# Row sums on one core: the first 2048 rows as two contiguous blocks, each with its own load and store

## The chip, the cores and the metric

One core of a Trainium2 chip. The metric is device time of one execution in microseconds (us). An execution counts as slow when it is over 1.5% above the fastest of its kernel, and else as fast. A profile's span is some 1.8 us shorter than the time, because the time also counts what lies around the program.

A load or a store is cut into packets, pieces that one of 16 DMA engines moves one after another. An instruction of SyncE or ScalarE issues it, and semaphores report its end.

## The reference

```python
batch, seq, dim = 32, 512, 1024
x = np.random.randn(batch, seq, dim).astype(np.float32)      # 67.1 MB
def reference(x):
    return np.sum(x, axis=-1).astype(np.float32)             # 16384 sums, 64 KB
```

There are 16384 rows of 4 KB. Each is read once, so the kernel is a stream of loads with a short head and a short tail.

## The kernel before

Rows are taken in groups of 2048: partition p of group g holds 16 neighbouring rows, one 64 KB run. VectorE sums most of them; near the end ScalarE takes some, and the last row comes in two pieces. The parts that matter here:

```python
BIG = 16
x_g = x.flatten_outer_dims().rearrange("(g p j) d -> g p j d", p=P, j=BIG)
out_v = out.rearrange("b s -> (b s)").rearrange("(g p j) -> p g j", p=P, j=BIG)
def rows_from(j, n):
    return x_g[j // BIG, :, j % BIG : j % BIG + n, :]
# ... (cut)
last = J // BIG - 1
FIRST = 4
# ... (cut)
        for g in range(last):
            t = inpool.tile([P, BIG * dim + 4], fp32)
            if g == 0:
                rows(t, 0, FIRST, 0, 0)                       # first load: 4 rows per partition
                first = sums_of[-1]
                rows(t, FIRST, BIG - FIRST, FIRST, 0)         # second load: the other 12
                continue
# ... (cut: the last group in pieces; `two` is the load of two rows per partition)
        hold(store(nc.scalar, 0, last), two, "its packets come behind those of the loads")
        halves(whole[:, :1], part)
        halves(sums[:, j : j + 1], whole)
        store(nc.sync, last, last + 1)
```

The first two loads together fill group 0, so each reads 128 runs (16 KB, then 48 KB) that start 64 KB apart; I call that distance the pitch. One store from ScalarE's queue writes the sums of the first seven groups, one from SyncE's queue those of the last. At the close SyncE waits for the ScalarE store, all engines meet at a barrier, and GpSimd, which also waits for the last store, clears the semaphores.

## Time and profile before

| | |
|---|---|
| time, median of 3 runs | 162.1 us (161.92 to 162.17) |
| span of the profiled execution | 159.6 us (its time was 161.4) |
| loads' queue, share of 16 DMA engines | 97.8% |
| first load landed | 7.14 us |
| last load landed, then end of span | 157.43 us, 2.2 us later |

### The profile page before, as it was taken

How to read it: one execution, taken by the hardware profiler on the slowest of the kernel's cores; microseconds unless marked ns; L12 is line 12 of the kernel's file. 1: busy time of each engine (PE TensorE's matmuls, PEld its weight loads, DVE VectorE, ACT ScalarE, POOL GpSimd, SP SyncE). 2: the span in 40 equal slices, each digit the busy share in tenths (PEclk: the TensorE clock that was granted, in tenths of full speed). 3: DMA queues.
4: the chain of work that ended last, by engine and by line, in shares of the span. 5: the costliest groups of instructions: out<-in, count | busy, mean ns of one | idle time of the engine just before them, and what ended most of it. 6: DMA issues, size and time to landing. Idle time of an engine off the chain costs nothing.

```text
span 159.6 us, 125 instructions
## 1 busy us (share of the span) xinstructions
DVE 120.1 (75%) x22; ACT 17.3 (11%) x31; POOL 0.2 (0%) x4
## 2 busy tenths in 40 slices
DVE  0290059960799958999499994999949999497953
ACT  3000000000000000000000000000000000496953
POOL 0000000000000000000000000000000000000000
DMA  7999996996996989979969969969969969798984
GB/s 263 460 406 579 394 526 263 526 526 263 526 526 263 526 378 411 526 312 476 526 279 509 526 263 526 526 263 526 526 263 526 509 279 526 337 452 371 467 365 128
DMA packets 2928, 67.18 MB, mean 421 GB/s; under 512 B 1264, under 2 KB 1392, under 8 KB 1520
## 3 DMA queue, kind: packets, MB, share of 16 engines
q1 hardware_dynamic: 2016, 67.12, 97.8%
q10 hardware_dynamic: 912, 0.06, 0.4%
HBM read 67.11 MB, written 0.07 MB: 421 GB/s over the span
## 4 chain that ended last, share of the span: by engine, by line
DMA 73%; DVE 25%; SPq 1%; issue 0%; DVEq 0%
DMA t<-in_x_dram 73%; DVE sums L141 24%; SPq L180 1%; SPq L221 0%; DVE t L155 0%; DVEq L252 0%
## 5 line engine op out<-in xcount | busy, mean ns | idle before, releaser
L141 DVE TENSOR_REDUCE sums<-t 128x16 f32<-128x16384 f32 (+3 forms) x9 | 116.6, 12954 | 35.3 <-DMA t<-in_x_dram 35.3
L168 ACT ACTIVATE unread<-t 128x1024 f32<-128x1024 f32 x15 | 15.2, 1012 | 139.2 <-DMA t<-in_x_dram 139.2
L155 DVE CUSTOM_DVE_ANT_0 t<-t 128x512 f32<-128x512 f32 (+2 forms) x6 | 3.5, 602 | 2.4 <-DMA t<-in_x_dram 2.4
L168 ACT ACTIVATION_READ_ACCUMULATOR unread<-t 128x1 f32 x15 | 2.8, 187 | 0.0
L168 ACT ACT_TABLE_LOAD x1 | 1.3, 1283 | 0.8 <-PEq L241 0.8
L155 DVE DVE_READ_ACCUMULATOR2_ANT sums<- 128x1 f32 x5 | 0.4, 83 | 0.0
L241 POOL MEMSET const-uint8-127<- 128x1 uint8 x1 | 0.1, 102 | 0.0
L241 POOL MEMSET const-bfloat16-1.0<- 128x1 bf16 x1 | 0.1, 101 | 0.0
L241 POOL MEMSET const-float32-0.0<- 128x1 f32 x1 | 0.1, 98 | 0.2 <-issue 0.2
L241 POOL MEMSET const-float32-1.0<- 128x1 f32 x1 | 0.1, 98 | 0.0
L155 DVE DVE_READ_ACCUMULATOR2_ANT t<- 128x1 f32 x1 | 0.1, 81 | 0.0
L219 DVE MEMSET t<- 128x1 f32 x1 | 0.1, 59 | 0.0
## 6 DMA issues: line engine op xcount, KB each, us to landing
t<-in_x_dram SPq DMA_DIRECT2D x1, 6144.0 KB, 20.9
t<-in_x_dram SPq DMA_DIRECT2D x1, 4096.0 KB, 31.1
t<-in_x_dram SPq DMA_DIRECT2D x1, 2560.0 KB, 36.9
t<-in_x_dram SPq DMA_DIRECT2D x1, 2048.0 KB, 7.1
t<-in_x_dram SPq DMA_DIRECT2D x1, 1024.0 KB, 38.9
t<-in_x_dram SPq DMA_DIRECT2D x1, 280.0 KB, 39.1
t<-in_x_dram SPq DMA_DIRECT2D x1, 232.0 KB, 39.2
t<-in_x_dram SPq DMA_DIRECT2D x6, 40.8
```

Source lines behind the costliest of these rows:

```text
L141: return nc.vector.tensor_reduce(out=dst, in_=src, axis=mybir.AxisListType.X, op=mybir.AluOpType.add)
L155: return nc.vector.tensor_tensor_reduce(out=src[:, :n], in0=src[:, :n], in1=src[:, n:], scale=1.0, scalar=0.0, op0=mybir.AluOpType.add, op ...
L168: nc.scalar.activation(out=unread[:, :n], in_=src, func=mybir.ActivationFunctionType.Copy, accum_out=dst,)
L180: load = nc.sync.dma_start(out=block, in_=rows_from(j, n))
L219: nc.vector.memset(whole[:, width + 1 :], 0.0)
L241: nc = _bacc.Bacc("TRN2", target_bir_lowering=False, num_devices=1)
```

## The change

The intent is that the first two loads read memory in one piece each: 4 neighbouring rows per partition in the first 512 rows, then 12 per partition in the next 1536. Their sums then belong to other places of the output, so the ScalarE store must be split in three. (`FIRST = 4` only moved up; `x_g` and `out_v` are the lines of before, written with `x_r` and `out_r`. The lines they replace are cut.)

```diff
+    FIRST = 4
+    x_r = x.flatten_outer_dims()
+    out_r = out.rearrange("b s -> (b s)")
+    x_g = x_r.rearrange("(g p j) d -> g p j d", p=P, j=BIG)
+    out_v = out_r.rearrange("(g p j) -> p g j", p=P, j=BIG)
+    blocks = ((0, FIRST), (FIRST, BIG - FIRST))
+    x_0 = [x_r[a * P : (a + n) * P].rearrange("(p j) d -> p j d", j=n) for a, n in blocks]
+    out_0 = [out_r[a * P : (a + n) * P].rearrange("(p j) -> p j", j=n) for a, n in blocks]
 
     def rows_from(j, n):
+        if j < BIG:
+            return x_0[blocks.index((j, n))]
         return x_g[j // BIG, :, j % BIG : j % BIG + n, :]
...
-        hold(store(nc.scalar, 0, last), two, "its packets come behind those of the loads")
+        behind = "its packets come behind those of the loads"
+        for (r, n), dst in zip(blocks, out_0):
+            hold(nc.scalar.dma_start(out=dst, in_=sums[:, r : r + n]), two, behind)
+        hold(store(nc.scalar, 1, last), two, behind)
```

More of the change, by code (lines that the diff above doesn't have):

```diff
@@ L117 @@
     BIG = 16
-    x_g = x.flatten_outer_dims().rearrange("(g p j) d -> g p j d", p=P, j=BIG)
-    out_v = out.rearrange("b s -> (b s)").rearrange("(g p j) -> p g j", p=P, j=BIG)
+    FIRST = 4
[6 more added lines that the diff above has]
+    out_0 = [out_r[a * P : (a + n) * P].rearrange("(p j) -> p j", j=n) for a, n in blocks]
     def rows_from(j, n):
+        if j < BIG:
+            return x_0[blocks.index((j, n))]
         return x_g[j // BIG, :, j % BIG : j % BIG + n, :]
     last = J // BIG - 1
-    FIRST = 4
     pieces = (560, 464)
```

## The prediction

> **What bounds the kernel now.** I read the page first (busy shares, the 40 slices, the DMA queues), then the chain of waits in order of time, then the waits, then groups by form, then the timeline of the last five microseconds, and at last the trace's single records of packets and of semaphore increments, because the change touches only the first and the last few microseconds.
>
> The page, parts 1 to 4: VectorE is busy 75% of the span, ScalarE 11%, while the loads' queue takes 97.8% of what 16 DMA engines have in the span. The chain that ends last is 73% loads.
>
> ```profile
> span 159.6 us, 125 instructions
> DVE 120.1 (75%) x22; ACT 17.3 (11%) x31; POOL 0.2 (0%) x4
> ...
> q1 hardware_dynamic: 2016, 67.12, 97.8%
> q10 hardware_dynamic: 912, 0.06, 0.4%
> ...
> DMA 73%; DVE 25%; SPq 1%; issue 0%; DVEq 0%
> ```
>
> The chain seems to give VectorE 25%, but that is only the time in which a load waited for its buffer; the DMA engines had another load queued meanwhile. The groups by form settle it: each 16-row reduction takes 17.22 us and there was idle time before the reductions, ended by a DMA each time.
>
> ```profile
> L141 DVE TENSOR_REDUCE sums<-t 128x16 f32<-128x16384 f32 x5 | 86.1, 17220 | 14.9 <-DMA t<-in_x_dram 14.9
> L141 DVE TENSOR_REDUCE sums<-t 128x12 f32<-128x12288 f32 x1 | 13.0, 12953 | 10.1 <-DMA t<-in_x_dram 10.1
> ```
>
> The packet records agree: the loads' packets per DMA engine sum to 155.91 us (5.48 for the 16 KB ones of the first load, 14.52 for the 48 KB ones of the second, 116.18 for the six loads of 64 KB runs, 19.73 for the last five), and they run from 1.015 to 156.93 us, which is 155.91 us. So the load queue never runs dry between its first packet and its last. Time can be won only by starting the first packet sooner, by shortening packets, or after 156.93 us.
>
> The timeline of the end shows what follows the last loads: a ScalarE-queue store of the first seven groups' sums, the last two short VectorE pieces, and the last store from the SyncE queue.
>
> ```profile
> 156.10 1.03 ACT L168 ACTIVATE unread<-t 128x1024 f32<-128x1024 f32 x1 [0.31 <-DMA t<-in_x_dram]
> ...
> 156.16 0.42 ACTq L191 DMA_DIRECT2D out_dram<-sums  x1
> ...
> 157.45 0.40 DVE L155 CUSTOM_DVE_ANT_0 t<-t 128x233 f32<-128x233 f32 x1 [0.16 <-DMA t<-in_x_dram]
> 157.78 0.08 DVE L155 DVE_READ_ACCUMULATOR2_ANT sums<- 128x1 f32 x1
> 157.89 0.35 SPq L191 DMA_DIRECT2D out_dram<-sums  x1
> ```
>
> The DMA issues give the time to landing of both stores:
>
> ```profile
> out_dram<-sums ACTq DMA_DIRECT2D x1, 56.0 KB, 2.1
> out_dram<-sums SPq DMA_DIRECT2D x1, 8.0 KB, 1.4
> ```
>
> The semaphore records are finer: the ScalarE store is complete at 158.29, SyncE's closing waits run from there, the barrier has gathered all engines by 158.99, and GpSimd's clear, which waits for the last store as well, is released by that store's 16th increment at 159.31; the span ends some 0.3 us later. So the closing barrier had 0.32 us to spare behind the last store. That slack is what the change eats.
>
> **What the Trainium skill says.** "DMA: Bandwidth & Descriptors", section Latency and other measured facts, row on HBM row pitch: a pitch of 512 KiB and more between the partitions' runs costs rate (207 GB/s at 512 KiB against 214 called full, 164 at 2 MiB), supposedly because lock-stepped streams fall on the same channels, and contiguous tiles are the remedy. The pitches here are 64 KB before (first two loads) and 16 and 48 KB after, all below that table. The trace before speaks against a steady loss: 48 KB packets at the 64 KB pitch take 1815 ns, which is 27.1 GB/s per engine, and the contiguous 64 KB packets take 2418 ns, also 27.1.
> The same page, section Where 436 GB/s comes from, sets a ceiling of 435.2 GB/s; 16 engines at 27.1 are 433, so the stream is at it already.
> The same page, section Issuing engines are not separate DMA queues: issuing from another engine only saves the sequencer's time. So the three ScalarE stores share the engines with the loads; their packets are few (0.55 us per engine before).
> "Perfetto Trace Analysis", section Per-instruction lifecycle: a DMA instruction's shown window is its issue alone, and the final semaphore write waits for the write's confirmation, which can take long to HBM. The trace agrees: the 0.42 us issue at 156.16 is complete 2.1 us after its start, the last packet having ended at 157.85, 0.44 us before.
>
> **The change part by part.** The order of instructions, built from both versions, has the same rows on VectorE, SyncE and GpSimd, and the same bytes in the same 128 descriptors for every load. Two things differ.
>
> (a) The first load reads 2 MB in one piece and the second 6 MB in one piece, where each was 128 runs at a 64 KB pitch. The second can win nothing, its packets being at the rate already. In the first load, the 16 packets that open the stream (one per engine) take 1151 ns on average and the next 16 take 654, against 611 for the rest. The whole excess is (685.1 - 611) x 8 packets = 0.59 us per engine. If it is an address conflict of 16 engines that start in step, contiguous rows may win up to that; if it is the cold start of the read path (latency, first pages), nothing. As the queue is never empty, whatever is won here moves everything after it, rigidly. I take 0.15 us as the expectation, about a quarter of what there is: the 48 KB packets at the same pitch show no excess, but their engines no longer start in step.
>
> (b) The one ScalarE store becomes three: 4 sums per partition, 12, and 6 x 16. All stand behind the last activation and are issued one after another by ScalarE's queue. First at 156.16 with the window of a 128-row store, 0.35, so until 156.51. The second needs its own semaphore wait first (0.05) beside the usual gap of 0.05, so it starts at 156.62; its window I take from the loads that are issued back to back in the chain of waits:
>
> ```profile
> 116.34 0.33 SPq L180
> 116.67 0.05 issue
> 116.72 0.43 SPq L180
> 117.15 0.05 issue
> 117.20 0.48 SPq L180
> ```
>
> A following issue takes 0.43 to 0.48 instead of 0.33. So the second lasts until 157.05, and the third, the large one, starts at 157.10. It lands 2.1 later, less 0.1 for one seventh fewer packets (7 x 128 packets spread over 0.75 us): 159.1 instead of 158.29. SyncE's closing waits include the semaphore of this third store, in the third of their pairs. From the landing to the gathered barrier took 0.70 us; two of the waits (0.13) will already be passed, so 0.57 + 0.03 remains: gathered at 159.7. The last store, issued at 157.89 as before, is still complete at about 159.3. So the clear starts at 159.7 instead of 159.34: +0.4 us. VectorE's two last pieces and the last store's issue are not touched.
>
> Sum: -0.15 + 0.4 = +0.25 us on 162.1, about 162.3 us.
>
> **The rivals.**
> 1. The opening packets are slow because of the 64 KB pitch, and contiguous rows cure it: up to -0.59 us, with the tail's +0.4 a net of -0.2, 161.9. For it: the excess sits only where all engines start in step. Against: the earliest packets take longest (1465 and 1389 ns) and the latest to start only 747, all finishing near 2.2 to 2.5 us, as if they all waited for one event, a cold start.
> 2. The stores' issue is hidden. If the three issues take 0.35 each, or the closing steps go faster, the third store lands by 158.8 and the tail costs 0.1 or nothing: 162.0 to 162.1 with the head's gain. Against: the slack is only 0.32 us, while two more issues cost at least 0.8.
> 3. The stores collide. Stores 1 and 2 send runs of 16 and 48 bytes as 256 further packets, the third's packets stand close before the last store's, which began at 158.73 before; if the last store slips behind them or short writes are slow to confirm, the end moves by up to 1 us: 163.0. Against: 57 packets per engine took 0.55 us, so 16 more cost about 0.16.
> 4. A contiguous first load is worse: 16 engines starting within 2 MB may meet in fewer channels. If the opening packets took twice their excess, +0.6: 162.9. Nothing in the profile speaks for it; the contiguous 64 KB runs of later loads are at full rate.
> A wait at a buffer is no rival: the first reduction ends at 11.6 us and the second at 34.6, and the load that needs it is wanted only at about 60.
>
> **Range and chances.** The steps span about -0.6 to +0.1 (rarely +0.6) at the head and 0 to +0.6 (rarely +1) at the tail. The runs before spread by 0.25 us. I put 161.7 to 162.9 for 8 in 10. A change of 2% is 3.2 us; no step reaches a third of it, so within 2% has 0.98, faster 0.01 and slower 0.01.
>
> **What would show it.** Right: the opening 16 packets still near 1.1 us on average and the first reduction starting between 6.6 and 7.2 us; every later reduction shifted by the same amount; three ScalarE-queue issues at about 156.2, 156.6 and 157.1; the third store landing after 159; the clear released by the barrier and no longer by the last store. Wrong: a first reduction before 6.6 us (rival 1) or after 7.3 (rival 4); a barrier gathered before the last store's landing (rival 2); the last store landing over 1.6 us after its issue (rival 3). A load queue that runs dry anywhere would break the whole argument.

## The result, and the profile after

The changed kernel takes 163.23 us (median of 6 runs, 163.06 to 163.59), the kernel before 162.08 (6 runs, 161.7 to 162.21). A ratio, here and below, is of fast runs over fast runs of the kernel before, with its 95% interval; it differs a little from a plain ratio of medians or means. Here it is 1.0076 (1.006 to 1.0092). The change costs 1.2 us, 0.8%. That is within 2%, but above the range that was stated (161.7 to 162.9).

The profiled execution after is the slowest of its six runs (163.59), and that of before (161.4) is faster than any of its six (161.7 to 162.21). The two traces are 2.2 us apart where the times are 1.2 apart, so differences read from this pair lean high. Its page, to be laid beside the one of before:

```profile
span 161.8 us, 128 instructions
...
q1 hardware_dynamic: 2016, 67.12, 96.6%
q10 hardware_dynamic: 1072, 0.06, 0.4%
```

The loads' packets and bytes are the same. The stores' queue has 160 more packets (912 to 1072), which is nothing in bytes. The two ends of the chain of waits, columns start, duration and what, first of the kernel before and then of the changed kernel:

```profile
0.00 7.14 DMA t<-in_x_dram
...
157.43 0.02 issue
```

```profile
0.00 8.09 DMA t<-in_x_dram
...
158.34 0.08 issue
```

The first load lands 0.95 us later and the last load 0.91 later: in this pair of traces, what was lost at the head is carried through the whole stream (another pair, below, loses half of it on the way). The rest is behind the last load: 2.2 us to the end of the span before, 3.47 after. The DMA issues of the changed kernel (queue, size, us from issue to landing) show where:

```profile
out_dram<-sums ACTq DMA_DIRECT2D x1, 48.0 KB, 2.7
out_dram<-sums ACTq DMA_DIRECT2D x1, 2.0 KB, 1.5
out_dram<-sums ACTq DMA_DIRECT2D x1, 6.0 KB, 1.6
out_dram<-sums SPq DMA_DIRECT2D x1, 8.0 KB, 2.2
```

The two small stores land quickly, but the large one takes 2.7 us (2.1 before, with more packets) and the last one 2.2 (1.4 before). The large store's last packet had ended 1.14 us before its landing (159.74, 160.89); before, 0.44 us. So the packets moved in time and their confirmation came late. The closing line's own instructions name the price: SyncE's waits, at most 28 ns each before, now contain one of 1524 ns, the wait for the large store (columns: count, then minimum, median and maximum ns; the kernel before first).

```profile
L252 SPq EVENT_SEMAPHORE  x6: 17/28/28, 158.3 to 159.6; - x6
L264 SPq EVENT_SEMAPHORE  x6: 17/28/1524, 159.3 to 161.8; - x6
```

So there are two losses, one at the head and one at the tail, and my two estimates for them were -0.15 and +0.4 us.

### The profile page after: what moved, and what is told of

It reads as the page before. It is cut to its first block, busy times and chain, and to the rows that moved or that the text cites. A ratio compares the mean times of both kernels' runs of the same rounds, so it can differ in the third digit from the quotient of the medians.

```text
span 161.8 us, 128 instructions
## 1 busy us (share of the span) xinstructions
DVE 120.0 (74%) x22; ACT 17.3 (11%) x31; POOL 0.2 (0%) x4
## 3 DMA queue, kind: packets, MB, share of 16 engines
q10 hardware_dynamic: 1072, 0.06, 0.4%
## 4 chain that ended last, share of the span: by engine, by line
DMA 73%; DVE 24%; SPq 1%; issue 0%; DVEq 0%
DMA t<-in_x_dram 73%; DVE sums L150 24%; SPq L189 1%; SPq L230 0%; DVE t L164 0%; DVEq L264 0%
```

## The experiments

Seventeen runs, in five sets. Kernels are compared only within the same rounds. "Landing" is the last of the 16 semaphore increments that a DMA makes, one per DMA engine. "End" is the time from the last load's landing to the end of the span. Times are medians.

### The two halves apart, and both kernels again

Loads alone (e1): contiguous loads, the old single store.

```diff
-        for (r, n), dst in zip(blocks, out_0):
-            hold(nc.scalar.dma_start(out=dst, in_=sums[:, r : r + n]), two, behind)
-        hold(store(nc.scalar, 1, last), two, behind)
+        hold(store(nc.scalar, 0, last), two, behind)
```

> The contiguous loads of the change with the single ScalarE store of before; rows 0 to 2047 come out in the wrong places on purpose. Theory (two parts): in the one trace of the changed kernel the slowest of the 16 DMA engines finished the first load 0.95 us later than before (landing 8.09 against 7.14), though the mean packet was only 14 ns longer; if the contiguous pattern causes that, this run is 0.5 to 1.0 us over before and its first load lands at 7.7 to 8.2. Rival (tail only: the late start was chance of that one execution): within 0.2 us of before, first landing 7.0 to 7.4.

Measured: 162.06 against 161.62 us, ratio 1.0017 (0.9998 to 1.0037). First landing 7.61 (just under the range expected), end 2.25 us. The means differ by 0.31 us, less than I expected and by itself not clear of the noise, but the late first landing is there and the end is as before.

Stores alone (e2): the loads of before, three stores.

```diff
-        hold(store(nc.scalar, 0, last), two, ...)
+        for r, n in ((0, FIRST), (FIRST, BIG - FIRST)):
+            hold(nc.scalar.dma_start(out=out_v[:, 0, r : r + n], in_=sums[:, r : r + n]), two, behind)
+        hold(store(nc.scalar, 1, last), two, behind)
```

> The loads of before with three ScalarE stores (right results; the two small stores write 16 and 48 bytes at a 64 byte pitch instead of contiguously). In the changed kernel's trace the span ended 3.47 us after the landing of the last load, before 2.21. Tail theory: 0.9 to 1.3 us over before, the third store landing at least 2.5 us after its issue. Head theory: at most 0.4 us over before.

Measured: 162.39 us, ratio 1.0036 (1.0014 to 1.0058), the means 0.60 us apart. Its trace, of its fastest run (161.98; the slowest was 162.76), has first landing 7.24, third store 2.03 us, end 2.66. Neither theory as written: three stores cost something, but the slow 2.7 us landing is not there. What is there is step (b) of the prediction, nearly to the number: the third issue 0.30 us ahead of the last load's landing (predicted 0.33), 2.03 us to its landing (2.0), an end of 2.66 (2.2 + 0.4). The tail has two parts.

The changed kernel again (e3) and the kernel before again (e4), unaltered:

> The changed kernel unaltered, for a second trace and to see how much of its late first landing (8.09) and of its late last landings (2.7 us for the third store, 2.2 for the last) is chance. If the pattern of addresses makes the head late: first landing again above 7.6. If chance: 7.0 to 7.4. Tail: if the stores' confirmation is slow by construction, third store again over 2.5 us from issue to landing; if chance, about 2.0. Time 1.0 to 1.3 us over before by either.

> The kernel before unaltered: gives the spread of a same kernel. Expected within 0.2 us of before, first landing 7.0 to 7.3, last landing to end 2.2 us. If the start of the DMA engines is a matter of chance, its first landing may be anywhere in 7.0 to 8.1.

Measured: the changed kernel 162.84 us, ratio 1.0071, first landing 7.80, large store 2.67, last store 2.10, end 3.33. The kernel before 161.76, ratio 1.0002, first landing 7.12, end 2.2. So both losses come back in a second trace. But of the 0.68 us between these two first landings only 0.31 is left at the last load (158.08 against 157.78). The kernel before against itself still spread from 161.40 to 162.25, and this bounds what one trace can prove.

### Loads crossed with stores

Beside its loads, e2 differed from the change in one thing: its small stores wrote 16 and 48 bytes at a 64 byte pitch, not contiguously. So I crossed them. Contiguous loads with strided small stores (e5), then old loads with contiguous ones (e6):

```diff
# e5
-        for (r, n), dst in zip(blocks, out_0):
-            hold(nc.scalar.dma_start(out=dst, in_=sums[:, r : r + n]), two, behind)
+        for r, n in blocks:
+            hold(nc.scalar.dma_start(out=out_v[:, 0, r : r + n], in_=sums[:, r : r + n]), two, behind)
# e6
-        if j < BIG:
-            return x_0[blocks.index((j, n))]
```

> The contiguous loads with the three stores of the tail-only run (small stores in 16 and 48 byte runs at a 64 byte pitch; wrong places on purpose). The slow end of the changed kernel (3.33 and 3.47 us from the last load's landing to the end, against 2.66 with three strided stores and 2.21 before). Theory: the contiguous small stores, where neighbouring runs share 64 bytes, make later writes slow to confirm; then here the end takes 2.6 to 2.7 and the third store 2.0 us. Rival: the loads' pattern or the engines' lag makes it; then 3.3 to 3.5 and the third store 2.6 to 2.8. Head by either theory: first landing 7.6 to 8.1.

> The loads of before with the changed kernel's three stores, small ones contiguous (wrong places on purpose). Theory of shared 64 bytes: third store 2.6 to 2.8 us from issue to landing, end 3.3 to 3.5 us after the last load's landing, whole about 1.0 us over before. Rival (loads' pattern): third store 2.0, end 2.7, whole 0.4 over before. Head by either: first landing 7.1 to 7.3.

The same view, the issues of the three ScalarE stores and the last one, for e5:

```profile
out_dram<-sums ACTq DMA_DIRECT2D x1, 48.0 KB, 2.0
out_dram<-sums ACTq DMA_DIRECT2D x1, 2.0 KB, 1.5
out_dram<-sums ACTq DMA_DIRECT2D x1, 6.0 KB, 1.6
out_dram<-sums SPq DMA_DIRECT2D x1, 8.0 KB, 1.5
```

and for e6:

```profile
out_dram<-sums ACTq DMA_DIRECT2D x1, 48.0 KB, 2.8
out_dram<-sums ACTq DMA_DIRECT2D x1, 2.0 KB, 1.5
out_dram<-sums ACTq DMA_DIRECT2D x1, 6.0 KB, 1.6
out_dram<-sums SPq DMA_DIRECT2D x1, 8.0 KB, 2.2
```

e5 and e6 differ in their loads too, so each is read beside its neighbours in this table; within a column only the places that the small stores write to differ between the last two rows, with the same packet counts and sizes. With contiguous small stores the large and the last store are late whatever the loads are.

| stores | loads of before: first landing, end, ratio | contiguous loads: first landing, end, ratio |
|---|---|---|
| one | 7.14, 2.2 | 7.61, 2.25, 1.0017 (e1) |
| three, small ones strided | 7.24, 2.66, 1.0036 (e2) | 7.83, 2.79, 1.0055 (e5) |
| three, small ones contiguous | 7.22, 3.41, 1.0055 (e6) | 7.80 and 8.09, 3.33 and 3.47, 1.0071 and 1.0076 |

Rows change the end, columns the first landing, and they add: e1 and e6 differ from before by 0.31 and 0.90 us in the means, 1.21 together, and the change by 1.16 (e3) and 1.24.

### Away from the end, and only the first load

The small stores issued as soon as their sums exist (e7, right results):

```diff
                 rows(t, FIRST, BIG - FIRST, FIRST, 0)
+                for (r, n), dst in zip(blocks, out_0):
+                    nc.scalar.dma_start(out=dst, in_=sums[:, r : r + n])
                 continue
...
-        for (r, n), dst in zip(blocks, out_0):
-            hold(nc.scalar.dma_start(out=dst, in_=sums[:, r : r + n]), two, behind)
         hold(store(nc.scalar, 1, last), two, behind)
```

> The changed kernel with the two small stores issued as soon as their sums are there (near 12 and 35 us; right results), so only the large ScalarE store is left at the end. Theory (two extra issues ahead of the third store and slow confirmation behind them make the tail): the end takes 2.1 to 2.3 us after the last load's landing, as before, and only the head's 0.5 to 0.9 us is left over before. Rival (contiguous loads alone make the tail slow): end still above 3. A further risk: their packets among the loads cost up to 0.2 us.

Measured: 162.03 us, ratio 1.0016, end 2.25, large store 2.0 us; what is left over before, 0.28 us in the means, is the head's. There the small stores themselves took over 20 us to land, their packets spread among those of the queued loads (the 16 byte ones from 15.8 to 31.0 us). That costs nothing, as nothing waits for them:

```profile
out_dram<-sums ACTq DMA_DIRECT2D x1, 48.0 KB, 2.0
out_dram<-sums ACTq DMA_DIRECT2D x1, 2.0 KB, 21.6
out_dram<-sums ACTq DMA_DIRECT2D x1, 6.0 KB, 23.2
```

Only the first load contiguous, the second as before, one store (e8): in `rows_from`, `if j == 0: return x_0[0]`.

> Only the first load is contiguous (16 KB pitch), the second at the 64 KB pitch, one store as before (wrong results on purpose). Theory: the pitch of the first load alone sets how late the slowest engine gets going; first landing 7.6 to 8.1, whole 0.4 to 0.9 over before. Rival (the second load's queueing behind it, or chance): first landing 7.1 to 7.3, whole within 0.2 of before.

Measured: first landing 7.80, ratio 1.0017 (0.9995 to 1.0038). The first load alone brings the late landing; the time is nearer to the rival's figure than to mine.

### Which short runs, and which pitch

Only one of the two small stores contiguous (e9, e10), old loads; for the other, `dst` is `out_v[:, 0, r : r + n]`.

> Loads of before, three stores, only the 48 byte runs contiguous, the 16 byte runs at a 64 byte pitch (wrong places on purpose; the two stores' ranges overlap). Theory A, runs of 48 bytes that straddle 64 byte lines make later stores slow to confirm: third store 2.6 to 2.8 us, end 3.3 to 3.5 us after the last load. Theory B, the 16 byte runs do (four in one line): third store 2.0 to 2.1, end 2.6 to 2.8.

> The counterpart: only the 16 byte runs contiguous, the 48 byte runs at a 64 byte pitch. Theory A: third store 2.0 to 2.1 us, end 2.6 to 2.8. Theory B: third store 2.6 to 2.8, end 3.3 to 3.5.

Both failed as experiments. The ranges of the two stores overlap: the build made the second store wait for the first one's landing. In e9 the second was issued at 158.59, after a landing at 158.51, and what came after ran late (ratios 1.0098 and 1.0084, third stores 2.05 and 2.08). They do not answer the question. (In e10 the 16 byte runs had landed, at 158.00, before the next store was issued, and the large store was not late.)

So I left one small store out altogether: no 16 byte runs (e13), no 48 byte runs (e14), by `for (r, n), dst in [(blocks[1], out_0[1])]` and the same with 0.

> Loads of before; of the small stores only the contiguous 48 byte one, then the large one; the first 512 sums are not written at all (wrong on purpose). No ranges overlap, unlike the two runs before, where the overlap made the second store wait for the first. If the 48 byte runs slow the later stores: third store 2.5 us or more from issue to landing, last store over 1.9. If the 16 byte runs do, or only both together: 2.0 to 2.1 and 1.4 to 1.5, end 2.2 to 2.5 us after the last load.

> The same with only the contiguous 16 byte store and then the large one; 1536 sums are not written (wrong on purpose). If the 16 byte runs slow the later stores: large store 2.5 us or more, last over 1.9. If the 48 byte runs do, or only both together: 2.0 to 2.1 and 1.4 to 1.5.

The store issues of e13, then of e14:

```profile
out_dram<-sums ACTq DMA_DIRECT2D x1, 48.0 KB, 2.0
out_dram<-sums ACTq DMA_DIRECT2D x1, 6.0 KB, 1.5
out_dram<-sums SPq DMA_DIRECT2D x1, 8.0 KB, 1.4
```

```profile
out_dram<-sums ACTq DMA_DIRECT2D x1, 48.0 KB, 2.8
out_dram<-sums ACTq DMA_DIRECT2D x1, 2.0 KB, 1.5
out_dram<-sums SPq DMA_DIRECT2D x1, 8.0 KB, 1.8
```

Ends 2.22 and 2.98, ratios 1.0024 and 1.0068. The contiguous 16 byte runs make the large store late: 2 KB of output in 128 writes, which land in 1.5 us themselves. The last store at 1.8 us stays under the 1.9 expected. One more issue ahead of the large store, without those runs, is hidden almost wholly by the end of e13; that e13's ratio is above 1 I cannot assign, since its trace lost 0.7 us in mid-stream, where it does not differ from the kernel before. e14's lost 0.5 us there, so its ratio is not the tail's alone either.

The order then matters. Large store first, then the 48 byte runs, then the 16 byte runs (e17, right results):

```diff
+        hold(store(nc.scalar, 1, last), two, behind)
-        for (r, n), dst in zip(blocks, out_0):
+        for (r, n), dst in reversed(list(zip(blocks, out_0))):
             hold(nc.scalar.dma_start(out=dst, in_=sums[:, r : r + n]), two, behind)
-        hold(store(nc.scalar, 1, last), two, behind)
```

> The changed kernel with its three ScalarE stores in the other order: large, 48 byte runs, 16 byte runs last (right results). If the contiguous 16 byte runs delay only what is written after them, the large store lands 2.0 to 2.2 us after its issue and the end comes 2.5 to 2.8 us after the last load (the third issue is still late, and the last store may be hit a little): 0.5 to 0.7 us less than the changed kernel. If short contiguous writes cost the same wherever they stand, the end takes 3.3 to 3.5 as in the changed kernel.

Measured: large store 2.21 us, last store 1.42, end 2.41, a little better than expected; time 162.01, ratio 1.0017 (1.0 to 1.0033). The issues, large store first:

```profile
out_dram<-sums ACTq DMA_DIRECT2D x1, 48.0 KB, 2.2
out_dram<-sums ACTq DMA_DIRECT2D x1, 6.0 KB, 2.0
out_dram<-sums ACTq DMA_DIRECT2D x1, 2.0 KB, 1.6
out_dram<-sums SPq DMA_DIRECT2D x1, 8.0 KB, 1.4
```

Three stores in this order cost little; most of the rest is the head's. One thing here limits the reading of e14: the last store was issued at 158.55, before the 16 byte runs had landed (159.53), and still took 1.42 us. So these runs do not delay every store behind them. Whether the last store of the changed kernel is late through them or through the late large store is open.

For the head, only the first load's pitch was varied. e11 does it for all loads: each partition takes 128 neighbouring rows, a 512 KB pitch, right results, one store of 448 byte runs. It was also my candidate for a faster kernel.

```diff
-    x_g = x.flatten_outer_dims().rearrange("(g p j) d -> g p j d", p=P, j=BIG)
-    out_v = out.rearrange("b s -> (b s)").rearrange("(g p j) -> p g j", p=P, j=BIG)
+    x_g = x.flatten_outer_dims().rearrange("(p g j) d -> g p j d", p=P, j=BIG)
+    out_v = out.rearrange("b s -> (b s)").rearrange("(p g j) -> p (g j)", p=P, j=BIG)
... (cut: the store helper indexes the new out_v)
```

The others replace `x_0[0]` in e8 by `x_r[: k * P].rearrange("(p j) d -> p j d", j=k)[:, :n, :]` with k = 17, 8 and 5 rows: 68, 32 and 20 KB.

> A candidate with right results: each partition takes 128 neighbouring rows, so all loads have a 512 KB pitch and the large store is 128 runs of 448 bytes in place of 896 of 64. If closeness of the opening reads makes the slow start, a wide pitch starts no later than before: first landing 6.9 to 7.2, whole 161.2 to 161.9. If power-of-two pitches alias[...] loads slow down: 64 KB packets over 2500 ns or first landing above 7.5, whole 162 to 200. Tail as before (slack hides the store), 2.1 to 2.3.

> Only the first load changed, to 4 of every 17 rows: a 68 KB pitch, no power of two (wrong results on purpose). Closeness theory: as the 64 KB pitch, first landing 7.1 to 7.3, whole within 0.2 us of before. Aliasing theory: 64 KB already pays for its power of two, so 6.6 to 7.0 here and the whole 0.2 to 0.5 less.

> Only the first load changed, to a 32 KB pitch (wrong results on purpose). If closeness of the opening reads makes the late start, and gradually: first landing between the 64 KB value (7.1 to 7.3) and the 16 KB one (7.6 to 8.1), near 7.4. If only touching rows matter: 7.1 to 7.3.

> Only the first load changed, to a 20 KB pitch: nearly as close as the contiguous 16 KB, but not contiguous and no power of two (wrong results on purpose). Closeness theory: 7.5 to 8.1. If contiguity or the power of two in the small pitch is what hurts: 7.1 to 7.3.

| pitch of the first load | first landing, us | ratio |
|---|---|---|
| 16 KB, contiguous (after, e1, e3, e5, e7, e8, e17) | 7.61 to 8.09 | 1.0017 where one store (e1, e8) |
| 20 KB (e16) | 7.75 | 1.0049 (1.0028 to 1.007) |
| 32 KB (e15) | 7.29 | 1.0001 |
| 64 KB (before, e2, e4, e6, e9, e10, e13, e14) | 7.11 to 7.24 | 1.0002 (e4) |
| 68 KB (e12) | 7.27 | 1.0013 (0.9985 to 1.0041) |
| 512 KB (e11) | 7.29 | 1.0004 (0.9983 to 1.0025) |

20 KB is neither contiguous nor a power of two and lands as late as 16 KB; 68 KB is no better than 64, and 512 no worse. So powers of two have no part in it, and of the theories only closeness of the runs fits every row, with the step between 20 and 32 KB. But 20, 32, 68 and 512 KB rest on one trace each, and e16 is late in another way than the 16 KB runs. With 16 KB the eighth of the first load's 16 increments comes at 7.25 to 7.31 us in all seven traces, against 6.89 to 7.06 with 32 KB and more: the typical engine is later. In e16 it comes at 6.87, and its packets are not slow (666.6 ns on average, 685.1 before); a few late engines alone make the 7.75, the last of which had its first packet only at 2.39 us. Its time is also 0.81 us over before in the means, where e8 is 0.29 over. That 16 and 20 KB are late for one reason is therefore not shown. The gradual version of the theory, which put 32 KB near 7.4, did not hold. The chain's first line of e16 and of e15:

```profile
0.00 7.75 DMA t<-in_x_dram
```

```profile
0.00 7.29 DMA t<-in_x_dram
```

No version here beats the kernel before; e11 equals it within the noise.

## Why the prediction was wrong

**The bound: right.** The stream of loads never ran dry: between 3 and 156 us fewer than 16 of its packets were under way for 0.4 us in all, in the trace before and in that after. (The prediction's own proof, 155.91 us of packets in 155.91 us, matches so exactly by luck: the engines' first packets start between 1.02 and 1.68 us, so packets must overlap a little.) The head's delay came out at the end in that pair of traces (0.95 us at the first landing, 0.91 at the last), by half between e4 and e3. VectorE's work, the packets and the number of DMA issues for loads stayed.

**The head, step (a): wrong in kind.** I took the mean excess of the opening packets over all engines, 0.59 us, as all that could be won, and guessed a quarter of it as gain. By that measure the changed kernel hardly differs: its 16 KB packets take 698.7 ns on average against 685.1, so the excess is 0.70 us per engine, 0.11 more. But a load has landed when the slowest of 16 engines has finished its eight packets. The last packet of the first load ended at 7.740 us against 6.785, while the first increments came at 7.03 and 6.77. After at most two opening packets each engine of this trace runs at 611 ns per packet, and the others take over nothing from the slowest: its lag was 1.06 us at the first load's landing and 1.01 at the last's. The pattern is rival 4, which I dismissed because the contiguous 64 KB runs of later loads are at full rate. Those runs are 64 KB apart; a run length and a pitch are not the same thing, and full rate in the one said nothing of a start at a 16 KB pitch. Its sign, written beforehand, showed: the first reduction started at 8.11 us, after 7.3. Why close runs delay this start is not shown; that 16 KB does, against 32 to 512 KB, is.

In time the head costs 0.3 us (0.31, 0.28 and 0.29 in the means of e1, e7 and e8; none clear of the noise alone, but they agree), less than the landings suggest. A likely reason, argued and not shown: in some traces 64 KB packets in mid-stream take over 2450 ns (144 of 768 in e13, 17 in e4, the kernel before; 1 to 3 in the traces of before, after, e2 and e3), and a kernel with one late engine hides part of such a delay in the others. From its first to its last landing e4 took 150.65 us and e3 150.28.

**The tail, step (b): right mechanism, one term mis-sized.** In e2, where the small stores are strided, the step comes out as written (end 2.66). In the changed kernel it does not. The third issue came 0.18 us ahead of the last load's landing; I had it 0.33 ahead, so it was 0.15 later. The clear was released by the barrier and no longer by the last store, as said: gathered at 161.45, the last store complete at 161.09. From the large store's landing to the gathered barrier took 0.56 us, against 0.57 plus a gap of 0.03. The failed term is "it lands 2.1 later, less 0.1": it took 2.72, and e2, e5 and e13 show that this term is 2.0 again when no contiguous 16 byte runs are written ahead of it. 0.15 and 0.72 are the 0.87 us by which the trace's end exceeds my 2.6. In time the tail costs 0.90 us (e6), of which the strided stores of e2 already cost 0.60, so the larger part is what step (b) foresaw, at 0.4. The contiguity is left with 0.30 (0.27 to 0.34 from e5 to the changed kernel), and the intervals overlap, so in time it is not clear of the noise; in the single traces the split is 0.45 and 0.75, also because e2's trace was of its fastest run.

**Rival 3** named short writes that are slow to confirm, and dismissed them by counting packets: their time on the engines (0.07 us for the 16 byte ones per engine) is indeed small. The cost was on the later stores' confirmation, which no busy share shows. Its sign showed too: the last store took 2.2 us, over 1.6. **Rivals 1 and 2** did not occur.

The chances were right (within 2%), but the range was built on a sum of two centred guesses, while both errors had the same sign: +0.45 at the head and +0.5 at the tail in time.

## What to carry to other kernels

When a transfer is spread over engines that do not share work, its end is that of the slowest engine, so read the last landing and not the mean packet. Contiguous in memory is no aim in itself: in this kernel a first load whose runs lay 16 or 20 KB apart landed later than one with runs 32 KB or more apart, and many tiny neighbouring writes made the large store after them late. If short stores are unavoidable, issue them early, when nothing waits for them, or behind the large ones.

## What the Trainium skill lacked or had wrong

- "DMA: Bandwidth & Descriptors", Latency and other measured facts: its row on pitch warns of powers of two from 512 KiB on. For these loads from HBM a 512 KB pitch cost nothing: 64 KB packets of 2418 ns at the median as before, ratio 1.0004 (e11). The row is about copies between HBM tensors (and about large powers of two; the prediction put it more widely as 512 KiB and more), so this bounds where it applies. It lacks the other end: pitches of 16 and 20 KB in a first load made it land at 7.61 to 8.09 us, against 7.11 to 7.29 for 32 KB and more.
- The same row offers contiguous tiles as a remedy for such large pitches. It says nothing of a 64 KB pitch, and there the contiguous first load was the one that landed later, 7.80 against 7.12 us in the same set (e3, e4).
- "DMA: Bandwidth & Descriptors", Specifications, says that transfers under 512 bytes are done by read-modify-write, but no page says that short writes which have landed in time themselves can make the next store's confirmation late: 128 contiguous writes of 16 bytes landed in 1.5 us, and the following 48 KB store took 2.8 us in place of 2.0 (e14 against e13). With a 64 byte pitch in place of contiguity it did not (e2 against e6, e5 against e3). That the read-modify-write is the mechanism, no run here shows.
- "DMA: Bandwidth & Descriptors", iDMA fabric, says in passing that a bulk load runs at the pace of its slowest engine. The traces agree, and had I used it, step (a) would have read another number. It lacks that the lag stays: in the changed kernel's trace it was 1 us both at the first landing (increments from 7.03 to 8.09) and 150 us later at the last load's (157.33 to 158.34).
